# Applying the inverse softmax sum of grouped heads after the product with V, in place of before it

## Chip, cores and metric

One core of a Trainium2 chip runs the whole program. The metric is the device time of one execution in microseconds, the median of several runs. A profiled execution gives, beside its time, the start and duration of every instruction on the engines: TensorE (PE, and PEld for its weight loads), VectorE (DVE), ScalarE (ACT), GpSimd (POOL), and SyncE (SP), which issues most of the transfers.

## What is computed

Two layers of a block with four parallel head groups (pooling, grouped-query attention, a long convolution called hyena, latent attention), an output projection and a mixture of experts with 16 experts. There are 512 latent tokens and 256 context tokens. Latent queries read keys of both, 768 in all; context queries, in the first layer only, read the 256 of the context. The part that matters here is the attention:

```python
def attend(q, k, v, scale):
    s = jnp.einsum('bqhgd,bkhd->bhgqk', q, k).astype(jnp.float32) * scale
    p = jax.nn.softmax(s, axis=-1).astype(v.dtype)
    return jnp.einsum('bhgqk,bkhd->bqhgd', p, v)

# in reference(), for each layer: four query heads of 64 on two key/value heads
o_gqa = block_sweep_attention(gqa_q(p_q, gqa_qnorm_g[l], pos),
                              jnp.concatenate([kl, kc], axis=1), jnp.concatenate([vl, vc], axis=1), gqa_scale)
...
mixed = jnp.concatenate([o_pool, o_gqa, o_hy, o_mla], axis=-1) @ w_out[l]
```

## The kernel before

Everything is f32, and where a matmul is to be fast, an operand is split into a high and a low half in a faster type (`split`, L715 to L721: ACT copies the high half, L718, and DVE subtracts it from the source, L721).

**Attention.** `attention` runs the grouped heads (kind "g") first and the latent heads (kind "m") after them, in two pairs of heads each; for a pair it goes over blocks of 128 queries, six in layer 0 (four latent, two context) and four in layer 1. One block of one pair is the generator `attend`, in three steps, and `step` keeps three blocks in flight: a new block does its first step, the block before it the second, the one before that the third.

The first step, `probs`, runs for each of the two heads: the scores by matmul into PSUM (L1116, two tiles of 1024 columns shared with hyena), the negated row maximum on DVE (L1118), the exponential on ACT with the row sum as its second output (L1121), the reciprocal of the sum on DVE (L1122), and then the scaling of the whole tile of probabilities P, 128x768 for latent queries and 128x256 for context queries. `SCALE_BY` gives the engine of that scaling by the block's number and the head: for grouped heads "vvpppv", where v is DVE (L1127) and p is POOL (L1125). The second step, `probs_t`, transposes P in pieces of 128x128 on PE (L1139) and evacuates them by ACT (L1144) or DVE (L1142). The third, at the end of `attend`, multiplies with V (L1064): the two heads of a pair stand side by side in one PSUM tile `po`, at partitions 0 and 64, with twelve matmuls for a latent block and four for a context block. The result, 128 feature rows by 128 queries, is split straight from PSUM into the tiles `oT` (L718, L721), which the output projection reads much later.

**Beside it.** The hyena chains (`hyena_chain`) are advanced between the blocks of the grouped heads. Each goes through PE (L1195, L1218), ACT (L1198), DVE and POOL (products and sums L1200 to L1212, dealt out by `HYENA_BY`; L1203, L1205 and L1206 are on POOL, L1204, L1207 and L1208 on DVE) and back to PE, and the two chains alternate. The rest of the transposed operands (L1073) and, in layer 0, the modulation of the next layer (L367, L375) run between them as well.

**Order.** The order in the code is not the order on the engines: the tile framework's planner places the instructions of each engine by a simulated timeline, except where `in_order` ties PE's. Every engine then runs its own queue in order.

**What the change touches.** `SCALE_BY`, the end of `probs` (L1120 to L1130), and `attend`. The buffers: P has four, the sums `sm` six, the small PSUM tiles (`ps1`: transposes, `po`, hyena) four.

Of the kernel before, what the change touches and what calls it, by code (L numbers as in the profile page):

```python
# [10 lines left out]
F32 = mybir.dt.float32  # L11
F32R = mybir.dt.float32r
U32 = mybir.dt.uint32
AF = mybir.ActivationFunctionType
OP = mybir.AluOpType
# [162 lines left out]
EARLY = 3, 9  # L178
LATE_STEPS = ((1, 0), (1, 2), (2, 0), (2, 2))

SCALE_BY = dict(g="vvpppv", m="vvpvpp")
EVACUATE_BY = dict(g="avaa", m="aaaa")
HYENA_BY = "pvppvvvppp"

# [21 lines left out]
class Block:  # L206
# [844 lines left out]
    def attend(self, p, kind, pair, i, ks, qs):  # L1051
        nc = self.nc
        kb = range(6) if i < 4 else range(4, 6)
        heads = (2 * pair, 2 * pair + 1)
        P = {h: self.probs(p, kind, qs[h], ks[h], i, h % 2, kb)
             for h in heads}
        yield
        pts = {h: self.probs_t(p, P[h], len(kb), kind, h % 2) for h in heads}
        yield
        po = self.ps1()  # L1060
        for j, b in enumerate(kb):
            for x, h in enumerate(heads):
                v = self.G[:, b, 64 * pair:64 * pair + 64] if kind == "g" else self.MV[:, b, 64 * h:64 * h + 64]
                nc.tensor.matmul(po[64 * x:64 * x + 64, :128], v, pts[h][:, j, :], start=j == 0, stop=j == len(kb) - 1,  # L1064
                                 tile_position=(0, 64 * x))
        c = slice(128 * i, 128 * i + 128)
        ob = (2 if kind == "g" else 6) + pair
        self.split(self.oT[0][ob][:, c], self.oT[1][ob][:, c], po[:, :128])

    def t_raw(self, srcs, w):  # L1070
        pt = self.ps1()
# [34 lines left out]
    def probs(self, p, kind, q, k, i, x, kb):  # L1106
        nc = self.nc
        k0, n = 128 * kb[0], 128 * len(kb)
        S = self.ps2()
        c = slice(128 * i, 128 * i + 128)  # L1110
        K = 128 if kind == "g" else 96
        terms = ((0, 0), (0, 1)) if kind == "g" else ((0, 0), (0, 1), (1, 0))
        for y, (a, b) in enumerate(terms):
            for s in range(0, n, 512):
                e = min(s + 512, n)
                nc.tensor.matmul(S[:, s:e], q[a][:K, c], k[b][:K, k0 + s:k0 + e], start=y == 0, stop=y == len(terms) - 1)  # L1116
        nm = self.work.tile([128, 1], F32, name="nm", tag="nm", bufs=6)
        nc.vector.tensor_reduce(nm, S[:, :n], axis=AX.X, op=OP.max, negate=True)  # L1118
        P = p.tile([128, NT], F32, name="P", tag="P", bufs=4)
        sm = self.work.tile([128, 1], F32, name="sm", tag="sm", bufs=6)  # L1120
        nc.scalar.activation(P[:, :n], S[:, :n], AF.Exp, bias=nm, accum_out=sm)  # L1121
        nc.vector.reciprocal(sm, sm)  # L1122
        e = SCALE_BY[kind][(2 * i + x) % 6]
        if e == "p":
            nc.gpsimd.tensor_scalar(P[:, :n], P[:, :n], sm, 1.0, op0=OP.mult, op1=OP.mult)  # L1125
        elif e == "v":
            nc.vector.tensor_scalar(P[:, :n], P[:, :n], sm, None, op0=OP.mult)  # L1127
        else:
            nc.scalar.activation(P[:, :n], P[:, :n], AF.Copy, scale=sm)
        return P  # L1130

    def probs_t(self, p, P, nk, kind, h):
        nc = self.nc
# [571 lines left out]
```

## Time and profile before

| | us |
|---|---|
| median of three runs | 1486.69 |
| lowest and highest | 1483.56, 1487.9 |
| profiled execution, its time | 1484.3 |
| its span, first to last instruction | 1482.4 |
| mean granted TensorE clock | 0.952 |

The page gives busy time and shares by engine; the queries of the trace give them by stretch, by line and along the chain that ended last. In the chain each piece is the work, or the time of the engine's queue ("issue"), that released what came after it. A line number is that of the kernel printed above.

### The profile page before, as it was taken

To read this page: it belongs to the slowest core of one execution; us is meant where nothing else is said; L and a number is where in the kernel's file an instruction comes from. 1 tells how busy PE (TensorE), PEld (TensorE's weight loads), DVE (VectorE), ACT (ScalarE), POOL (GpSimd) and SP (SyncE) were. 2 spreads that over 40 slices of the span, in tenths; PEclk is the share of its full clock that TensorE was granted. 3 is DMA by queue.
4 is the path that set the end of the run, shared out by engine and by line. 5 is a ranking of instruction groups with operands and counts; after the bars stand their busy time and mean duration, and the time that the engine had idled before them with its cause. 6 is when DMAs were issued, how large, how long until landed. Compare 5 with 4: busy or idle time off the path is not lost.

```text
span 1482.4 us, 23909 instructions
## 1 busy us (share of the span) xinstructions
PE 1345.9 (91%) x9457; PEld 888.8 (60%) x9457; DVE 684.3 (46%) x1831; ACT 507.1 (34%) x1238; POOL 341.9 (23%) x360
## 2 busy tenths in 40 slices
PE   6999999888899998999999968988899974998896
PEld 2577787777678895444444437977778961332221
DVE  4656364687663547122222227585787452221111
ACT  4545333435564433111111136544357430111000
POOL 1510141254210115121222132042521011111101
PEclk9989999999899998999999989999999986999998
DMA  9546746011265139899999980123100858999996
GB/s 386 220 159 243 278 156 245 31 58 43 79 264 170 58 128 350 341 395 392 396 392 398 386 283 5 61 83 139 57 30 3 350 203 326 406 393 409 405 402 215
DMA packets 72737, 345.96 MB, mean 233 GB/s; under 512 B 7105, under 2 KB 23105, under 8 KB 38322
## 3 DMA queue, kind: packets, MB, share of 16 engines
q1 hardware_dynamic: 57488, 305.24, 52.3%
q0 software_dynamic: 13104, 32.19, 8.0%
q10 hardware_dynamic: 2034, 7.00, 1.2%
q8 instruction: 75, 1.23, 0.3%
q14 instruction: 36, 0.29, 0.1%
HBM read 317.70 MB, written 26.71 MB: 232 GB/s over the span
## 4 chain that ended last, share of the span: by engine, by line
PE 74%; DVE 9%; DMA 9%; ACT 3%; issue 3%; POOL 1%; POOLq 0%; ACTq 0%; DVEq 0%; SPq 0%
PE b L1622 13%; PE b L808 7%; PE b L1655 6%; PE b L1633 4%; PE b L1116 3%; PE b L367 3%; PE b L797 3%; PE b L798 3%; PE b L799 3%; PE b L1064 3%; DMA ring<-wu 3%; PE b L1304 3%; PE b L1306 3%; PE b L1305 3%; PE b L1139 3%
## 5 line engine op out<-in xcount | busy, mean ns | idle before, releaser
L1622 PE MATMUL b<-ring,xg 128*64 128x512 f32 x824 | 222.4, 618 | 13.5 <-DMA ring<-wu 10.6
L1622 PEld LDWEIGHTS b<-ring,xg 128*64 128x64 f32 x824 | 66.9, 141 | 130.5 <-issue 103.1
L1608 ACT ACTIVATE sgl<-b 64x512 f32<-64x512 f32 x32 | 18.9, 591 | 345.9 <-PE b L1622 345.9
L1655 PE MATMUL b<-ring,hTm 128*64 128x512 f32 x464 | 110.9, 605 | 2.0 <-DVE hTm L1649 1.3
L797 PE MATMUL b<-whi,hT 128*128 128x256 f32 (+1 forms) x352 | 103.1, 294 | 0.3 <-DVE h L769 0.3
L798 PE MATMUL b<-wlo,hT 128*128 128x256 f32 (+1 forms) x352 | 100.3, 285 | 0.0
L799 PE MATMUL b<-whi,hT 128*128 128x256 f32 (+1 forms) x352 | 99.9, 284 | 0.0
L1116 PE MATMUL b<-kop,qop 96*128 96x512 f32 (+3 forms) x360 | 86.1, 370 | 13.5 <-ACT P L1121 10.8
L808 PE MATMUL b<-hT,whi 128*128 128x512 f32 (+1 forms) x384 | 96.3, 357 | 1.5 <-DVE cv L864 1.3
L721 DVE TENSOR_TENSOR wlo<-ringt,whi 128x256 fp32r<-128x256 f32 (+1 forms) x192 | 83.0, 474 | 30.1 <-ACT whi L718 29.7
L1649 DVE COPY hTm<-b 128x384 f32<-128x384 f32 (+1 forms) x32 | 15.7, 491 | 164.0 <-PE b L1646 98.3
L718 ACT ACTIVATE whi<-ringt 128x256 fp32r<-128x256 f32 (+1 forms) x192 | 67.5, 404 | 47.6 <-PE b L808 22.4
L1601 POOL DMA_INDIRECT xs<-y,sidx x32 | 50.2, 1568 | 135.0 <-DVE y L1599 131.5
L1121 ACT ACTIVATE P<-b,nm 128x768 f32<-128x768 f32 (+1 forms) x80 | 65.4, 818 | 38.9 <-DVE nm L1118 37.2
L1118 DVE TENSOR_REDUCE nm<-b 128x1 f32<-128x768 f32 (+1 forms) x80 | 67.1, 845 | 23.1 <-PE b L1116 22.4
L797 PEld LDWEIGHTS b<-whi,hT 128*128 128x128 f32 x352 | 68.4, 195 | 12.3 <-issue 3.7
L1116 PEld LDWEIGHTS b<-kop,qop 96*128 96x128 f32 (+1 forms) x360 | 58.5, 201 | 25.2 <-ACT P L1121 14.0
L808 PEld LDWEIGHTS b<-hT,whi 128*128 128x128 f32 x384 | 63.2, 188 | 15.3 <-ACT oT L1263 2.1
L1304 PE MATMUL b<-whi,oT 128*128 128x256 f32 x240 | 71.3, 299 | 0.0
L798 PEld LDWEIGHTS b<-wlo,hT 128*128 128x128 f32 x352 | 68.7, 195 | 3.2 <-issue 2.5
L1655 PEld LDWEIGHTS b<-ring,hTm 128*64 128x64 f32 x464 | 32.7, 138 | 60.9 <-issue 57.4
L1144 ACT ACTIVATE PT<-b 128x384 f32<-128x384 f32 (+1 forms) x140 | 57.3, 448 | 34.4 <-PE b L1139 33.5
(398 smaller groups left out, 2881.1 us busy)
## 6 DMA issues: line engine op xcount, KB each, us to landing
ring<-wd SPq DMA_DIRECT2D x58, 1024.0 KB
ring<-wu SPq DMA_DIRECT2D x53, 1024.0 KB
ring<-wg SPq DMA_DIRECT2D x50, 1024.0 KB
ringt<-wmod SPq DMA_DIRECT2D x46, 1024.0 KB
ringt<-win SPq DMA_DIRECT2D x14, 1024.0 KB
ringt<-wg SPq DMA_DIRECT2D x14, 1024.0 KB
ringt<-wu SPq DMA_DIRECT2D x11, 1024.0 KB
ringt<-wout SPq DMA_DIRECT2D x8, 1024.0 KB
```

The costliest lines, as they stand in the source:

```text
L718: nc.scalar.activation(hi, src, AF.Copy)
L721: nc.vector.tensor_tensor(lo, src, hi.bitcast(F32), op=OP.subtract)
L797: nc.tensor.matmul(pt[:, :n], hT[0][:, k, t], hi[k], start=k == 0, stop=False)
L798: nc.tensor.matmul(pt[:, :n], hT[0][:, k, t], lo[k], start=False, stop=False)
L799: nc.tensor.matmul(pt[:, :n], hT[1][:, k, t], hi[k], start=False, stop=k == 7)
L808: nc.tensor.matmul(pt[:, a:b], w[k][:, cs], hT[h][:, k, a:b], start=first and k == 0, stop=end and k == 7)
L1116: nc.tensor.matmul(S[:, s:e], q[a][:K, c], k[b][:K, k0 + s:k0 + e], start=y == 0, stop=y == len(terms) - 1)
L1118: nc.vector.tensor_reduce(nm, S[:, :n], axis=AX.X, op=OP.max, negate=True)
L1121: nc.scalar.activation(P[:, :n], S[:, :n], AF.Exp, bias=nm, accum_out=sm)
L1304: nc.tensor.matmul(pt[:, :256], oT[0][k][:, t], hi[k], start=k == 0, stop=False)
L1622: nc.tensor.matmul(pa[64 * j:64 * j + 64], X[:, k, o:o + 64], w[k // 4][:, c], start=k == 0, stop=k == 7, tile_position=(0, 64 * j))
L1655: nc.tensor.matmul(py[64 * j:64 * j + 64], hT[:, f], wd[f // 2][:, d:d + 512], start=f == 0, stop=f == 3, tile_position=(0, 64 * j))
```

## The change

For grouped heads the probabilities stay as the exponential leaves them. `probs` returns the reciprocal of the sum beside P. After the product with V, one matmul a head writes the reciprocals, spread over 64 rows, into columns 128 to 255 of the same PSUM tile: the stationary operand is the column of 128 reciprocals repeated 64 times, the moving one the identity, so that each output row holds the reciprocals of the 128 queries. ACT copies that spread tile into SBUF (`rsb`), DVE multiplies the product with V by it into SBUF (`on`), and the split reads `on` in place of PSUM. The latent heads keep their scaling; their line of `SCALE_BY` has only v and p, so that the branch for ACT goes.

```diff
-SCALE_BY = dict(g="vvpppv", m="vvpvpp")
+SCALE_BY = "vvpvpp"
...
-        P = {h: self.probs(p, kind, qs[h], ks[h], i, h % 2, kb)
-             for h in heads}
+        P, sums = {}, {}
+        for h in heads:
+            P[h], sums[h] = self.probs(p, kind, qs[h], ks[h], i, h % 2, kb)
...
-        self.split(self.oT[0][ob][:, c], self.oT[1][ob][:, c], po[:, :128])
+        o = po[:, :128]
+        if kind == "g":
+            for x, h in enumerate(heads):
+                nc.tensor.matmul(po[64 * x:64 * x + 64, 128:256], sums[h].to_broadcast([128, 64]), self.ident,
+                                 start=True, stop=True, tile_position=(0, 64 * x))
+            r = p.tile([128, 128], F32, name="rsb", tag="rsb", bufs=2)
+            nc.scalar.activation(r, po[:, 128:256], AF.Copy)
+            o = p.tile([128, 128], F32, name="on", tag="on", bufs=2)
+            nc.vector.tensor_tensor(o, po[:, :128], r, op=OP.mult)
+        self.split(self.oT[0][ob][:, c], self.oT[1][ob][:, c], o)
...
-        sm = self.work.tile([128, 1], F32, name="sm", tag="sm", bufs=6)
+        sm = self.work.tile([128, 1], F32, name="sm", tag="sm", bufs=8)
...
-        e = SCALE_BY[kind][(2 * i + x) % 6]
+        if kind == "g":
+            return P, sm
+        e = SCALE_BY[(2 * i + x) % 6]
...
-        else:
-            nc.scalar.activation(P[:, :n], P[:, :n], AF.Copy, scale=sm)
-        return P
+        return P, sm
```

## Rows read from the trace of the kernel before

**Rows 1.** The page, busy time, share of the span and instructions of each engine.

```profile
PE 1345.9 (91%) x9457; PEld 888.8 (60%) x9457; DVE 684.3 (46%) x1831; ACT 507.1 (34%) x1238; POOL 341.9 (23%) x360
```

**Rows 2.** Stretches: us, busy and count of PE, PEld, DVE, ACT, POOL; granted clock, DMA.

```profile
280.00:320.00 40.00, 34.88 (x244) 30.95 (x243) 32.98 (x61) 19.45 (x41) 20.92 (x18) 0.91 0.09 27
320.00:360.00 40.00, 31.93 (x224) 26.95 (x223) 34.09 (x71) 15.51 (x44) 21.31 (x26) 0.92 0.24 79
360.00:400.00 40.00, 33.48 (x265) 28.39 (x264) 27.45 (x68) 20.29 (x56) 11.63 (x18) 0.87 0.08 28
400.00:440.00 40.00, 39.64 (x357) 29.47 (x357) 23.93 (x60) 28.17 (x75) 5.06 (x7) 1.00 0.68 260
...
1080.00:1100.00 20.00, 18.61 (x131) 16.15 (x131) 15.77 (x31) 12.09 (x28) 6.67 (x7) 0.83 0.16 54
1100.00:1120.00 20.00, 19.84 (x191) 17.08 (x192) 15.30 (x34) 14.65 (x37) 1.51 (x2) 1.00 0.01 2
```

**Rows 3.** Stretches, DVE scaling L1127 alone: us, busy and count, clock, DMA.

```profile
285.00:394.00 109.00, 7.86 (x12) 0.89 0.15 49
1040.00:1105.00 65.00, 7.15 (x10) 0.90 0.12 43
```

**Rows 4.** The same for the POOL scaling L1125.

```profile
300.00:392.00 92.00, 8.65 (x12) 0.91 0.16 53
1050.00:1098.00 48.00, 5.84 (x6) 0.93 0.13 45
```

**Rows 5.** The chain that ended last: start us, us, what.

```profile
299.11 0.54 DVE P L1127
...
327.19 1.42 issue
...
336.97 1.45 PE b L1064 x22
...
347.32 0.53 DVE P L1127
...
1046.74 0.54 DVE P L1127
...
1076.35 1.43 issue
...
1103.77 0.53 DVE P L1127
...
1117.05 1.46 PE b L1064 x24
```

**Rows 6.** Timeline, DVE and POOL: start us, us, engine, line, operation, tiles.

```profile
300.62 0.67 DVE L1207 TENSOR_TENSOR layt<-layt 128x512 f32<-128x512 f32 x1
...
327.06 1.63 DVE L1127 TENSOR_SCALAR P<-P,sm 128x768 f32<-128x768 f32 x1
328.24 1.57 POOL L1206 TENSOR_TENSOR layt<-layt 128x512 f32<-128x512 f32 x1
328.81 1.55 DVE L1207 TENSOR_TENSOR layt<-layt 128x512 f32<-128x512 f32 x1
...
354.88 2.06 POOL L1125 TENSOR_SCALAR P<-P,sm 128x768 f32<-128x768 f32 x2
355.03 1.02 DVE L1208 TENSOR_TENSOR layt<-layt 128x256 f32<-128x256 f32 x1
355.98 1.11 DVE L1211 TENSOR_TENSOR hyscr<-hyscr 128x128 f32<-128x128 f32 x2
357.88 0.48 DVE L1211 TENSOR_TENSOR layt<-layt 128x128 f32<-128x128 f32 x2
```

**Rows 7.** Groups by line and form, 285 to 412 us: busy us, mean ns, idle before.

```profile
L1118 DVE TENSOR_REDUCE nm<-b 128x1 f32<-128x768 f32 x24 | 22.6, 950 | 3.8 <-PE b L1116 3.5
...
L721 DVE TENSOR_TENSOR oT<-b,oT 128x128 fp32r<-128x128 f32 x12 | 3.4, 282 | 2.9 <-ACT oT L718 2.9
L718 ACT ACTIVATE oT<-b 128x128 fp32r<-128x128 f32 x12 | 3.3, 278 | 10.0 <-PE b L1064 10.0
```

More of the change, by code (lines that the diff above doesn't have):

```diff
@@ L1119, in probs @@
         P = p.tile([128, NT], F32, name="P", tag="P", bufs=4)
-        sm = self.work.tile([128, 1], F32, name="sm", tag="sm", bufs=6)
+        sm = self.work.tile([128, 1], F32, name="sm", tag="sm", bufs=8)
         nc.scalar.activation(P[:, :n], S[:, :n], AF.Exp, bias=nm, accum_out=sm)
         nc.vector.reciprocal(sm, sm)
-        e = SCALE_BY[kind][(2 * i + x) % 6]
+        if kind == "g":
+            return P, sm
+        e = SCALE_BY[(2 * i + x) % 6]
         if e == "p":
             nc.gpsimd.tensor_scalar(P[:, :n], P[:, :n], sm, 1.0, op0=OP.mult, op1=OP.mult)
-        elif e == "v":
+        else:
             nc.vector.tensor_scalar(P[:, :n], P[:, :n], sm, None, op0=OP.mult)
-        else:
-            nc.scalar.activation(P[:, :n], P[:, :n], AF.Copy, scale=sm)
-        return P
+        return P, sm
     def probs_t(self, p, P, nk, kind, h):
```

## The prediction

> **What bounds the kernel now.** I read the busy shares first [rows 1]: PE 91%, DVE 46%, ACT 34%, POOL 23%. An average over stages, it says only that whatever is put on PE is paid somewhere. The change touches the grouped heads, which run at about 290 to 406 us in layer 0 and 1035 to 1119 us in layer 1, so the second view is busy time by stretch [rows 2]. From 280 to 360 us DVE is busy 33 and 34 of 40 us while PE has 5 and 8 us idle: there DVE and the hyena chain, which shares its queue, set the pace. From 360 to 400 us PE idles 6.5 us, and from 400 us on PE is full. Layer 1 repeats it: 15.8 of 20 us of DVE with PE at 18.6 from 1080 to 1100 us, PE full from 1100 us. POOL is half busy at most. So the same microsecond is worth something on DVE early in the grouped heads and on PE late in them. What it is worth is read from the third view, the chain that ended last: a piece of work that isn't on it gives nothing when it goes.
>
> The grouped heads take 20 blocks (two pairs of heads, six blocks of queries in layer 0 and four in layer 1), 40 scalings in all.
>
> **Removed: 22 scalings on DVE.** They take 7.86 us (12) and 7.15 us (10), 15.0 us [rows 3]. On the chain stand only 11 of them: five in layer 0, 2.57 us together, and six in layer 1, 2.89 us (the first and the last of each layer in [rows 5]). Term: -5.5 us. With the order of the work unchanged this is also the most that their own time can give.
>
> One of the 22, at 327 us, ran beside POOL's hyena products and took 1.63 us in place of about 0.6; its like in layer 1 did the same, and the chain carries 1.42 and 1.43 us there as "issue" [rows 5, 6]. That wait goes too, but what is late next stands close by: POOL's product L1206 ends at 329.8 us and DVE's L1208 needs it, while L1207, the last piece ahead of L1208, ends at 330.4 now [rows 6]. So I take 0.5 us at each place, -1.0 us; ends 0 and -2.85.
>
> **Removed: 18 scalings on POOL.** 8.65 us and 5.84 us [rows 4], none on the chain. Their worth is what they slow on DVE: two of them at 354.9 to 356.9 us stand beside L1208 (1.02 us) and the pair L1211 (1.11 us) [rows 6]. The pair took 0.48 us when the scalings were over, 0.63 less, and I give L1208 as much. Both are on the chain: -1.2 us; ends 0 and -1.3. The reciprocal stays, and all waits around it.
>
> **Added on PE: two matmuls a block.** The stationary operand is the column of inverse sums spread over 64 columns, the moving one the identity, 128 columns, f32: the shape of the product with V. There a block of 12 matmuls shows as 24 instructions and lasts 1.46 us [rows 5], 61 ns each, with the two heads side by side in the array. Two more are four instructions, 0.244 us a block, 4.9 us for 20. The product with V is on the chain in 12 of the 20 blocks (nine pieces in layer 0, four in layer 1; the first and the last in [rows 5]): +2.9 us; ends 0, if they run in PE's gaps, and +4.9. A zero-stride stationary operand I price as any other.
>
> **Added on DVE: one product a block.** 128x128, one source in PSUM, as the subtraction of the split now: 282 ns [rows 7], 5.6 us for 20. I give it the chain share of what it replaces in the same queue, 5.5 of 15.0 or 36%: +2.0 us; ends +0.6 (about a tenth, which is what the existing subtractions have on the chain) and +5.6. Net, DVE has 15.0 - 5.6 = 9.4 us less to do.
>
> **Moved: the subtraction of the split.** It read PSUM and one SBUF tile; now it reads two SBUF tiles. No 128x128 row of that kind stands in these stretches; the nearest is L1207, two SBUF sources of 128x512, which took 0.67 us at 300.6 us, where POOL stood idle, and 1.55 us beside POOL's L1206 [rows 6], 0.9 more. The subtractions that stand beside or just ahead of hyena products are four (about 321, 329, 1070 and 1078 us). Term: four times 0.9 by a chain share between a tenth and 36%, the larger: +1.3, cut to +1.0 because a scaling that took the same wait is gone from two of these places; ends 0 and 4 x 1.57 = +6.3, a whole POOL product each.
>
> The Trainium skill, SBUF — State Buffer, section Who interferes with whom, says that a DVE instruction with two SBUF inputs contends with a GpSimd instruction that reads SBUF, that one of them then blocks for the other's whole instruction, and that with at most one SBUF input it doesn't contend outside the two-port modes. By that the subtraction loses a freedom that it has now, and the sum would take the upper end in place of +1.0. The rows agree in kind (L1207), and not that every such place costs a whole POOL instruction: 0.9 us of 1.57 there.
>
> **Added on ACT: one copy a block**, PSUM to SBUF, 278 ns as the copy of the split [rows 7], 5.6 us in all. ACT is busy 20 us or less of 40 to 400 us and 15 of 20 in the last stretch of layer 1 [rows 2], so I take 0; ends 0 and, with the 12 blocks of the chain, +3.3. The copy that makes the high half changes its source to SBUF and keeps 278 ns.
>
> **Added waits.** Before: PE, ACT copy, DVE subtraction. After: PE, ACT copy, DVE product, ACT copy, DVE subtraction. DVE's product waits for ACT where the subtraction waited before, so that costs nothing new. New is that the second ACT copy waits for the DVE product, and behind it in ACT's queue stand the next exponentials (L1121) and the evacuations of the transposed probabilities (L1144), for which PE waits. No such wait is in this trace; from 0 to one row maximum, 0.95 us [rows 7], a block. I take 0, since the planner puts work between such a pair, and keep the other end for a rival. The output tiles themselves are read only by the output projection, long after. The sums live two steps longer; eight buffers for the six alive leave no wait. No DMA is added or moved, and SP's queue is passed by nothing.
>
> **Sum.** -5.5 - 1.0 - 1.2 + 2.9 + 2.0 + 1.0 = -1.8 us. After the grouped heads PE is full through the other heads and the projection, and the expert loads of layer 1 start when the last attention tiles are free, so a gain is carried to the end. Against the profiled execution, 1484.3 us with a span of 1482.4, that is 1482.5; that execution lies 2.4 us under the median of the runs, 1486.7. Against the median it gives **1484.9 us**. All gains at their ends and PE's and DVE's additions at the low ones: -5.5 - 2.85 - 1.3 + 0.6 = -9.1, 1477.6 us.
>
> **Rivals.** *Relief in full.* DVE is the pace until PE's last long stall is over, about 380 us and 1092 us, so PE's additions fall into idle time until there, and of the 12 chain blocks only the eight later than that pay: 8 x 0.244 = 2.0. With DVE's product at its low end and no contention: -5.5 - 2.0 - 1.2 + 2.0 + 0.6 = -6.1, about 1480.5 us. For it: DVE at 84% beside PE at 80 to 87% [rows 2]. Against it: the scalings have only a third of their time on the chain.
> *Held ACT queue.* The second copy waits behind whatever DVE does. With one row maximum ahead of the product, 0.95 us, in the 12 chain blocks, at DVE's 84% busy: 12 x 0.95 x 0.84 = +9.6, net +7.8, about 1494.5 us, slower. It decides from about 0.55 us of held ACT in each of the 12 blocks (6.3 us, which takes back the 1.8 and costs 4.5). For it: the strict order of ACT's queue and DVE at 84% early. Against it: ACT idles half of the early stretch, and late DVE is at 69 to 77% [rows 2].
> *Port wait in full.* The subtraction at its upper end: -1.8 - 1.0 + 6.3 = +3.5, about 1490.2 us. The skill's rule above is this mechanism. Against it: four places of 20, and the planner can put them elsewhere.
> That the change doesn't do what it says has no case: the scalings go by a plain return.
>
> **How the numbers follow.** What a measurement here can tell from no change is about 0.3%, 4.5 us: faster is below 1482.2, slower above 1491.2. Forecast 0.44, with a range of its own of 1481 to 1488.5, of it 0.05 below 1482.2; relief in full 0.28, faster; held ACT 0.20, slower; port wait 0.08, same. Faster 0.05 + 0.28 = 0.33, same 0.39 + 0.08 = 0.47, slower 0.20. The range of 1478 to 1494 takes in the low end of the sum nearly and about half of the held queue, and leaves out some 0.1 to 0.15.
>
> **What would show it.** Right: scalings of grouped heads gone from DVE and POOL, 80 new PE instructions at about 61 ns apart; DVE from 280 to 360 us down from 67 to about 63 of 80 us; PE's idle from 280 to 400 us 1 to 3 us smaller; the grouped heads' last product with V at most 3 us earlier per layer. Wrong: an ACT gap of over 0.5 us ahead of the second copy in most blocks (held queue); subtractions of over 1 us (port); or a different order of hyena and attention, which moves PE's long stalls and the stretches at a granted clock of 0.87 to 0.92 [rows 2]: the planner sees other work and may place all of it anew, and no row of before prices that.

## The result and the profile after

The changed kernel takes 1494.8 us (median of six runs, 1490.4 to 1499.1) against 1484.5 us for the kernel before: a ratio of 1.0064, 95% interval 1.0046 to 1.0082. It is slower by 0.64%, and 0.8 us above the upper end of the predicted range. The profiled execution ran 1494.4 us with a span of 1492.6, 10.2 us more than that of before.

The page of the changed kernel: busy time of each engine (answers to [rows 1]), and the engines' shares of the chain that ended last.

```profile
PE 1351.9 (91%) x9537; PEld 893.3 (60%) x9537; DVE 675.9 (45%) x1829; ACT 512.4 (34%) x1258; POOL 328.4 (22%) x342
...
PE 69%; DMA 12%; DVE 10%; ACT 4%; issue 3%; POOL 1%; POOLq 0%; SPq 0%; ACTq 0%; DVEq 0%
```

DVE and POOL do less (8.4 and 13.5 us), PE has the 80 new instructions, ACT 20 copies more. The change does what it says. The stretches of [rows 2] in the changed kernel, with the columns given there:

```profile
280.00:320.00 40.00, 34.25 (x241) 30.49 (x240) 31.93 (x59) 19.99 (x42) 16.04 (x14) 0.91 0.09 27
320.00:360.00 40.00, 31.42 (x235) 26.41 (x234) 31.44 (x67) 16.69 (x47) 19.59 (x21) 0.91 0.23 79
360.00:400.00 40.00, 33.38 (x254) 28.84 (x253) 24.69 (x65) 19.00 (x54) 9.92 (x14) 0.83 0.08 27
```

From 280 to 360 us DVE fell from 67.1 to 63.4 of 80 us, as promised. But PE did not close up behind it: its idle time from 280 to 400 us is 20.95 us, and was 19.7.

To see where the 10 us came in, I measured four lengths in each trace: **A0** and **A1**, from the first score matmul to the first projection matmul of layers 0 and 1 (the attention stages, with the hyena chains); **T0**, from the last projection matmul of layer 0 to the first matmul of its experts (the routing, its last loads, the late filter); and **S**, from the first score matmul of layer 0 to the end. Single executions of one kernel spread by over 10 us (the kernel before ran between 1477.5 and 1492.6 us in one set of rounds), much of it ahead of the first score matmul and in the expert stages. Between the two traces that the kernels before and after each have, A0 and T0 differ by at most 0.3 us, A1 by at most 1.1. So the steps below are read from these lengths, and the ratio stands beside them. All kernels of the study, lengths in us from one trace each, ratio to the kernel before from 6 to 12 runs:

| kernel | A0 | T0 | A1 | S | ratio (95%) |
|---|---|---|---|---|---|
| before, two traces | 177.7, 177.4 | 37.5, 37.5 | 123.5, 122.4 | 1195.2, 1194.4 | 1.0014 (1.0000 to 1.0028) |
| after, two traces | 182.4, 182.3 | 42.9, 42.9 | 123.6, 123.6 | 1205.4, 1202.2 | 1.0064 and 1.0058 (1.0035 to 1.0081) |
| after_order_of_before | 178.7 | 41.4 | 123.0 | 1197.0 | 1.0023 (1.0000 to 1.0047) |
| before_order_of_after | 183.1 | 40.2 | 126.7 | 1208.5 | 1.0086 (1.0056 to 1.0116) |
| relief_in_order | 173.7 | 37.5 | 119.7 | 1183.7 | 0.9946 (0.9928 to 0.9964) |
| add_in_order | 180.0 | 39.4 | 125.5 | 1197.7 | 1.0021 (1.0004 to 1.0039) |
| psum_in_after_order | 183.7 | 45.2 | 124.6 | 1204.9 | 1.0071 (1.0042 to 1.0099) |
| psum_in_order | 179.0 | 37.9 | 122.3 | 1193.5 | 1.0015 (0.9997 to 1.0034) |
| after_tail_of_before | 182.0 | 41.9 | 123.5 | 1200.2 | 1.0036 (1.0016 to 1.0055) |
| before_tail_of_after | 177.4 | 40.5 | 122.3 | 1193.5 | 0.9992 (0.9973 to 1.0012) |
| after_pe_order | 179.7 | 39.5 | 122.6 | 1201.6 | 1.0060 (1.0040 to 1.0079) |
| after_dve_order | 179.1 | 40.5 | 126.4 | 1198.1 | 1.0059 (1.0032 to 1.0085) |
| after_hyena_order | 182.5 | 41.4 | 123.5 | 1203.9 | 1.0083 (1.0052 to 1.0113) |
| before_other_split | 177.9 | 39.8 | 124.6 | 1198.0 | 1.0025 (1.0009 to 1.0041) |
| rec_in_order | 184.2 | 37.4 | 125.2 | 1204.1 | 1.0041 (1.0018 to 1.0063) |
| rec_free | 181.4 | 40.3 | 124.9 | 1202.5 | 1.0077 (1.0048 to 1.0106) |
| early_in_order | 187.3 | 40.2 | 127.3 | 1209.1 | 1.0088 (1.0064 to 1.0112) |

The kernel before against itself came out at 1.0014 (up to 1.0028), so a ratio of that size tells nothing. The second line is the loss: A0 +4.8, T0 +5.4, A1 +0.7 against the means of before, and 0.8 us given back in the experts of layer 0 (from their first matmul to the last of the main down projection 274.3 us, against 274.8 and 275.3). Half of it lies in T0, where not one instruction was edited. But the lengths don't all arrive at the end: before_tail_of_after has 3.0 us more in T0 than before and the time of before (0.9992, S 1193.5), and after_pe_order has 2.7 and 3.4 us less in A0 and T0 than the changed kernel and its ratio (1.0060).

### The profile page after: what moved, and what is told of

It is laid out like the page before. It is cut to its first block, busy times and chain, and to the rows that moved or that the text cites. A ratio compares the mean times of both kernels' runs of the same rounds, so it can differ in the third digit from the quotient of the medians.

```text
span 1492.6 us, 24054 instructions
## 1 busy us (share of the span) xinstructions
PE 1351.9 (91%) x9537; PEld 893.3 (60%) x9537; DVE 675.9 (45%) x1829; ACT 512.4 (34%) x1258; POOL 328.4 (22%) x342
## 4 chain that ended last, share of the span: by engine, by line
PE 69%; DMA 12%; DVE 10%; ACT 4%; issue 3%; POOL 1%; POOLq 0%; SPq 0%; ACTq 0%; DVEq 0%
PE b L1632 10%; PE b L808 7%; PE b L1665 5%; DMA ring<-wg 4%; PE b L1643 4%; DMA ring<-wu 4%; PE b L1126 3%; PE b L367 3%; PE b L1065 3%; PE b L797 3%; PE b L798 3%; PE b L799 3%; PE b L1149 3%; PE b L1314 2%; PE b L1315 2%
## 5 line engine op out<-in xcount | busy, mean ns | idle before, releaser
L1632 PE MATMUL b<-ring,xg 128*64 128x512 f32 x824 | 217.5, 605 | 16.4 <-DMA ring<-wu 12.5
L1126 PE MATMUL b<-kop,qop 96*128 96x512 f32 (+3 forms) x360 | 84.1, 366 | 13.2 <-ACT P L1131 11.1
L797 PEld LDWEIGHTS b<-whi,hT 128*128 128x128 f32 x352 | 68.5, 195 | 12.4 <-issue 3.7
L1128 DVE TENSOR_REDUCE nm<-b 128x1 f32<-128x768 f32 (+1 forms) x80 | 66.8, 844 | 19.6 <-PE b L1126 18.8
L1126 PEld LDWEIGHTS b<-kop,qop 96*128 96x128 f32 (+1 forms) x360 | 57.9, 199 | 24.2 <-ACT P L1131 13.6
L799 PEld LDWEIGHTS b<-whi,hT 128*128 128x128 f32 x352 | 68.6, 195 | 0.8 <-issue 0.8
```

What stands on the lines that cost most here:

```text
L797: nc.tensor.matmul(pt[:, :n], hT[0][:, k, t], hi[k], start=k == 0, stop=False)
L799: nc.tensor.matmul(pt[:, :n], hT[1][:, k, t], hi[k], start=False, stop=k == 7)
L1632: nc.tensor.matmul(pa[64 * j:64 * j + 64], X[:, k, o:o + 64], w[k // 4][:, c], start=k == 0, stop=k == 7, tile_position=(0, 64 * j))
```

## The experiments

Three theories stand against each other. **Theory 1**: the planner, seeing other work, places untouched instructions anew, and that order costs the time. **Theory 2**: the subtraction of the split, now with two SBUF operands, waits beside POOL. **Theory 3**: the second ACT copy, waiting for DVE's product, holds ACT's queue.

**Order apart from work.** Both kernels share all instructions but the 40 scalings and the new ones, and write them down in the same sequence before the planner sorts them. So the order that it gave to one kernel can be held in the other, by order-only dependencies along each engine's list; the instructions that only one kernel has are left to the planner.

```diff
+                end = self.replay(f"A{l}")
                 self.attention(l, pp, ag, hy, hyena_done, mla_out, last, side)
                 side.drain()
+                end()
...
+            for e, runs in REPLAY.get(key, {}).items():
+                order = [own[e][a + j] for a, k in runs for j in range(k)]
+                for prev, i in zip(order, order[1:]):
+                    self.tc.add_manual_dep(i, prev.name, mybir.DependencyInfo(
+                        mybir.DependencyClass.NoSync, mybir.DependencyReason.DATA), reason="in order")
```

REPLAY holds the lists as runs (first place in the written sequence, count), for the attention stages of both layers (A0, A1) and for the stretch from the projection of layer 0 to its experts (P0).

> The changed kernel with the instructions that both kernels have held in the order of the kernel before on PE, DVE, ACT and POOL, in the attention stages of both layers and in the stretch between projection and experts of layer 0; only the new instructions (spread, copy, product) are placed by the planner. What is left is the price of the change's own instructions and waits. Theory 1 (order is most of the loss): close to my sum, 1483 to 1487, ratio 0.999 to 1.0015. Theory 2 (the subtraction with two SBUF sources waits beside POOL, 2.3 us in layer 0, and PE's own additions of 0.24 us per block for about ten blocks where PE is full): 1487 to 1490, ratio 1.0015 to 1.0035. Theory 3 (the second ACT copy holds ACT's queue, in 20 blocks): the whole loss of the grouped-head stages stays whatever the order, and the time is that of the run with the tail's order alone, 1489 to 1492, ratio 1.003 to 1.005.

> The kernel before, with its own scalings of the probabilities and none of the new instructions, but with all other instructions of the attention stages and of the stretch behind the projection of layer 0 in the order of the changed kernel on PE, DVE, ACT and POOL. Theory 1: it is as slow as the changed kernel or nearly so, 1490 to 1495, ratio 1.0037 to 1.007. Theories 2 and 3, by which the new instructions themselves cost the time: 1484 to 1486 if only the tail is neutral too, and at most 1490 with the tail's 5.3 us.

The first came out at 1.0023, the second at 1.0086. The attention stage of layer 0 in both kernels (columns as in [rows 2]), the changed kernel in the order of before first:

```profile
288.40:467.00 178.60, 157.24 (x1314) 128.97 (x1313) 120.00 (x280) 97.31 (x268) 52.74 (x64) 0.94 0.33 116
```

```profile
283.70:466.80 183.10, 158.44 (x1267) 129.73 (x1265) 124.41 (x282) 95.12 (x257) 62.44 (x76) 0.92 0.32 114
```

The second kernel has the work of before, to the instruction (PE x1267, POOL x76), and is 5.6 us longer in A0 than the kernel before, by order alone; the first has the work of the changed kernel (x1314) and is 1.1 us longer than before. Theory 1 stands for A0: of its 4.8 us, 3.7 are order. In layer 1 the order of after costs 3.7 us with the work of before, and 0.6 us with the work of the changed kernel. No run holds a kernel in its own order without another edit, so what the holding costs by itself isn't measured; the nearest is psum_in_after_order below, with A0 1.3 us longer than in the changed kernel.

How the order costs can be read from A0 of the changed kernel and of the kernel before (second trace):

```profile
287.20:469.70 182.50, 160.88 (x1316) 132.36 (x1314) 120.81 (x280) 98.20 (x267) 53.94 (x64) 0.92 0.32 114
282.60:460.00 177.40, 156.99 (x1267) 128.53 (x1265) 123.16 (x280) 94.78 (x255) 62.21 (x76) 0.93 0.33 117
```

In the changed kernel PE is busy for 160.9 us in its own order and for 157.2 in the order of before, with the same matmuls, while its idle time is the same within 0.3 us. What differs is the granted clock: 27.4 us of A0 lie at 0.50 (1.2 GHz, the lower of its two levels) in the one, 21.1 in the other. So the 3.7 us are not longer waits but slower work; 6.3 us more at half speed are worth about 3.2 us of work, an estimate from these rows. In us, two traces averaged where there are two:

| kernel | A0 | PE busy | PE idle | of A0 at 0.50 |
|---|---|---|---|---|
| before | 177.5 | 157.1 | 20.4 | 23.9 |
| after | 182.4 | 160.7 | 21.7 | 27.4 |
| after_order_of_before | 178.7 | 157.3 | 21.4 | 21.1 |
| before_order_of_after | 183.1 | 158.5 | 24.7 | 28.5 |
| relief_in_order | 173.7 | 154.4 | 19.2 | 20.5 |
| add_in_order | 180.0 | 157.4 | 22.6 | 18.8 |

With the work of before, the other order costs mostly idle time (4.3 of 5.6 us). That the clock is the way in which the order costs is read from traces; no run changed the clock alone.

**The two halves of the change, in the order of before.**

```diff
-        if kind == "g":
-            with self.added():
-                for x, h in enumerate(heads):
...
-                nc.vector.tensor_tensor(o, po[:, :128], r, op=OP.mult)
```

> The changed kernel without spread, copy and product, so that the grouped heads stay unnormalised; all other instructions held in the order of the kernel before in the attention stages of both layers and behind the projection of layer 0. It measures the removed scalings by themselves. My sum has 7.7 us for them (5.5 on the chain, 1.0 beside POOL, 1.2 of slowed hyena steps). If they were on the path: ratio 0.994 to 0.997, and the two grouped-head stretches together 6 to 8 us shorter than 177.7 + 123.5 us. If the hyena chain or the fixed order of PE ends each step anyway: ratio 0.9985 to 1.001, and the stretches at most 2 us shorter.

```diff
-        if kind == "g":
-            return P, sm
-        e = SCALE_BY[(2 * i + x) % 6]
+        e = SCALE_BY[kind][(2 * i + x) % 6]
+        with self.added() if kind == "g" else ExitStack():
```

> The changed kernel with the old scalings kept as well, so that the grouped heads are normalised twice; all instructions of the kernel before held in its order. It measures spread, copy, product and the split from two SBUF sources by themselves. My sum: +5.9 us (2.9 PE, 2.0 DVE, 1.0 subtraction), ratio 1.003 to 1.005, upper end with the port wait in full +11, ratio 1.0075. If an instruction placed in a fixed order mostly falls into idle time: +1 to +3 us, ratio 1.0005 to 1.002. If the held ACT queue matters (the second copy of ACT behind DVE's product, 20 blocks): idle time of ACT before that copy of over 0.5 us a block and a ratio of 1.005 or more.

The two stages of the first (removal alone), then of the second (additions alone):

```profile
283.10:456.80 173.70, 154.46 (x1268) 126.60 (x1266) 115.51 (x268) 94.98 (x255) 53.37 (x64) 0.94 0.34 120
1023.20:1143.00 119.80, 109.66 (x936) 95.06 (x934) 85.33 (x166) 71.51 (x172) 34.84 (x32) 0.96 0.15 51
```

```profile
287.40:467.40 180.00, 157.43 (x1315) 128.79 (x1313) 125.72 (x292) 97.97 (x269) 61.48 (x76) 0.95 0.33 116
1034.70:1160.20 125.50, 113.55 (x967) 97.97 (x966) 93.98 (x184) 73.93 (x179) 40.38 (x38) 0.95 0.18 62
```

The removal gives 3.9 + 3.2 = 7.1 us, the additions cost 2.5 + 2.6 = 5.1 us. That is my sum, nearly: 7.7 and 5.9. Added up they make -2.0 us, but both together, in the same order, came to +1.1 in A0 and +0.1 in A1. So 3.2 us don't add, 2.5 of them in A0. The table above shows where: PE's idle time does add (-1.2 and +2.2 make +1.0, and +1.0 was measured); its busy time doesn't (-2.7 and +0.3 against +0.2), since removal and additions, each alone, also shortened the time at the lower clock level, by 3.4 and 5.1 us, and both together by only 2.8. So in this place most of what the removal alone, and the additions alone, seem to be worth is the clock that they met.

**The port wait.** In the changed kernel DVE's product and subtraction in layer 0 stand as follows (count, then least, median and most ns):

```profile
L1077 DVE TENSOR_TENSOR on<-b,rsb x12: 276/282/292, 319.3 to 412.7; 128x128 f32<-128x128 f32 x12
L721 DVE TENSOR_TENSOR oT<-on,oT x12: 277/282/1374, 321.0 to 414.4; 128x128 fp32r<-128x128 f32 x12
```

Two subtractions took 1.37 and 1.34 us beside POOL's hyena products; in the kernel before they took 0.28 [rows 7]. With the product in PSUM one of its operands leaves SBUF:

```diff
-                o = p.tile([128, 128], F32, name="on", tag="on", bufs=2)
+                o = po[:, 256:384]
```

> The changed kernel in its own order (held on PE, DVE, ACT and POOL in the attention stages and behind the projection of layer 0), with one edit: DVE writes its product into PSUM, so that the subtraction of the split reads one operand from SBUF and not two. In the traces of the changed kernel that subtraction took 1.37 and 1.34 us in place of 0.28, twice in layer 0, while POOL worked on the hyena tables. Theory 2 (the port wait costs up to 2.3 us of the 4.8 that the grouped-head stage of layer 0 grew by): the two long subtractions fall to about 0.28 us and the stage from 182.4 to 180 to 180.5 us. If the wait lies beside other work, and order is the cause: the long subtractions go, the stage stays at 181.7 to 182.6 us, ratio 1.004 to 1.007.

> The changed kernel with the product in PSUM as in the run beside it, and the shared instructions held in the order of the kernel before, as in the run with the order of before (178.7 us in the stage of layer 0, 123.0 in that of layer 1, 41.4 behind the projection; 177.7, 123.5 and 37.5 in the kernel before). There the subtraction was lengthened three times, to 0.7 us. Theory 2: 0.5 to 1.5 us less over both stages. If it is beside other work: the same within 0.3 us. Ratio 0.999 to 1.002, and the stretch behind the projection anywhere from 37.5 to 42 us, since it goes by where a DVE operation meets one of POOL there.

The same line in the changed kernel's own order, with the product in PSUM:

```profile
L772 DVE TENSOR_TENSOR oT<-b,oT x12: 276/281/292, 323.0 to 417.8; 128x128 fp32r<-128x128 f32 x12
```

The long subtractions are gone, all 12 under 0.3 us, and A0 is 183.7 us, not shorter than 182.4. In the order of before the same edit changes A0 by +0.3 and A1 by -0.7. Theory 2 falls. Yet both waits stand on the changed kernel's chain that ended last:

```profile
321.08 1.30 DVE oT L721
...
330.28 1.27 DVE oT L721
```

With the product in PSUM the next hyena step on DVE comes no sooner, since it waits for POOL's product, or is slowed beside POOL itself:

```profile
324.31 0.69 DVE L1270 TENSOR_TENSOR hyscr<-hyscr 128x512 f32<-128x512 f32 x1 [0.98 <-POOL hyscr L1268]
...
333.47 1.74 DVE L1270 TENSOR_TENSOR layt<-layt 128x512 f32<-128x512 f32 x1 [0.31 <-POOL layt L1268]
```

The first of these steps starts 35.0 us behind the first score matmul, and 35.1 in the changed kernel; the second takes 1.74 us in place of 0.68. The wait for POOL is there either way, on one instruction or on the next: standing on the chain is not yet a price.

**The held ACT queue** needs no run of its own. ACT's waits for DVE's product in A0 (us in total, times, longest), in the changed kernel:

```profile
ACT oT L718 <- DVE on L1077: 4.8, 5, 1.8
```

and in the changed kernel in the order of before:

```profile
ACT oT L769 <- DVE on L1129: 10.8, 12, 2.5
```

The kernel with more than twice the wait, 0.9 us in each of 12 blocks, has the shorter stage, by 3.7 us. So Theory 3 falls as the cause of the loss. What these waits are worth beside the 1.1 us that are left in the order of before, no run took apart.

**Which place of the order.** Three kernels hold part of it: PE alone; DVE, ACT and POOL alone; and 74 PE instructions around the second round of the hyena chains.

```diff
+REPLAY = {"A0": {"PE": [(99, 3), (114, 4), (75, 1), (102, 4), (76, 6), (142, 16), (106, 4), (118, 12), (158, 9), (130, 12), (167, 3)]}}
```

(the last of the three is shown, the others hold the whole lists of their engines in A0 and A1)

> The changed kernel with PE alone held in the order of the kernel before, in the attention stages of both layers; DVE, ACT and POOL are placed by the planner. It tells which engine's order cost the stage of layer 0 its 3.7 us (182.4 us in the planner's order, 178.7 in the order of before on all engines). If PE's order does (scores and transposes of heads put ahead of hyena's transforms, or behind them): 178.5 to 179.5 us. If the order of DVE, ACT and POOL does: 181.5 to 183 us. Between the two if both take part.

> The changed kernel with DVE, ACT and POOL held in the order of the kernel before, in the attention stages of both layers; PE is placed by the planner. If the order of these three engines cost the 3.7 us: 178.5 to 179.5 us in the stage of layer 0. If PE's order did: 181.5 to 183 us.

> The changed kernel with 74 PE instructions of layer 0 held in the order of the kernel before, and nothing else: those around the second round of the hyena chains. In the traces the changed kernel has the hyena product that opens this round ready 1.6 us earlier than the kernel before, and its transform on PE then starts 2.0 us later, since the planner put scores, transposes and AV matmuls of the attention ahead of it. If this place is where the order costs the stage of layer 0 its 3.7 us: 178.7 to 180 us (182.4 in the changed kernel, 178.7 with the whole order of before, 179.7 with PE's whole order). If the loss is spread over the later re-placements: 181.5 to 182.5 us.

The place looked plain in the traces. PE in the changed kernel, from the product that closes the first hyena round (start us, us, line, operation, tiles; L1195 transposes the chain's input, L1205 is its transform, L1126 scores, L1149 transposes of the probabilities):

```profile
304.39 3.66 PE L1228 MATMUL b<-ringt,layt 128*128 128x256 f32 x14 [0.49 <-DVE layt L1221]
307.70 1.05 PE L1126 MATMUL b<-kop,qop 128*128 128x512 f32 x4
308.59 0.49 PE L1149 MATMUL b<-cst,P 128*128 128x128 f32 x3
308.91 0.64 PE L1195 MATMUL b<-cst,cv 128*128 128x128 f32 x4
310.30 2.27 PE L1205 MATMUL b<-hyscr,ringt 128*128 128x128 f32 x18 [0.75 <-ACT hyscr L1196]
312.42 0.63 PE L1195 MATMUL b<-cst,cv 128*128 128x128 f32 x4
312.89 1.15 PE L1149 MATMUL b<-cst,P 128*128 128x128 f32 x9
313.87 1.73 PE L1205 MATMUL b<-hyscr,ringt 128*128 128x128 f32 x14
```

The changed kernel in the order of before (here L1247, L1257, L1178 and L1201; its first score matmul is 1.1 us later):

```profile
306.48 0.59 PE L1280 MATMUL b<-ringt,layt 128*128 128x256 f32 x2
306.91 0.63 PE L1247 MATMUL b<-cst,cv 128*128 128x128 f32 x4
307.38 2.76 PE L1280 MATMUL b<-ringt,layt 128*128 128x256 f32 x12
309.97 3.73 PE L1257 MATMUL b<-hyscr,ringt 128*128 128x128 f32 x32
```

The transform of the second round ends at 315.60 us in the one, 313.70 in the other: counted from the first score matmul 28.4 and 25.3 us. In the one, four scores and three transposes of the attention stand ahead of the round and nine transposes inside it; in the other it runs through. Yet holding this place alone brought nothing (A0 182.5), since DVE and POOL stood in the new order and the later rounds lost as much. Holding PE's whole order brought 2.7 us of 3.7, holding that of the other three 3.3. The loss isn't one misplaced group; either engine's order, held, pulls most of the rest along. Neither made the program faster than the changed kernel (1.0060 and 1.0059); the order of all engines, in all three stretches, did (1.0023). After_dve_order is 2.8 us longer in A1 than the changed kernel.

**The stretch behind the projection.** Two kernels run once more with no edit, and two exchange their order in this stretch alone:

```diff
+REPLAY = {
+    "P0": {
...
+        "Pool": [(0, 1), (2, 1), (1, 1), (3, 12), (17, 3), (22, 5), (15, 1), (27, 1), (16, 1), (28, 3), (20, 2)],
```

> The kernel before once more, with no edit, for a second trace. In its first trace the stretch from the last projection matmul of layer 0 to the first matmul of the experts took 37.5 us; in five other kernels of this study it took 40.2 to 42.9, in whatever order it stood. Theory A, 37.5 is this kernel's own length and the change adds 3 to 5 us there by something that is not the order: 37 to 38.5 us again. Theory B, the length of this stretch differs from one execution to the next and the first trace was a short one: 39 to 42 us, and the median of the timed runs as for the kernel before, ratio 0.998 to 1.002.

> The changed kernel once more, with no edit, on the chip and in the rounds of the others, so that all ratios stand against the same runs. Expected of both theories: ratio 1.005 to 1.008; in the trace the stretch from the first score matmul to the first projection matmul of layer 0 takes 182 to 183 us again (177.7 in the kernel before). By theory B on the stretch behind the projection, its 42.9 us may come out anywhere from 39 to 43.

> The changed kernel, with one thing fixed: between the output projection and the experts of layer 0 each engine's instructions stand in the order that the planner gave them in the kernel before (they are the same instructions in both kernels; in the changed kernel the planner pulled one POOL scaling of xh ahead of three sums of the late filter, and two PE transposes ahead of eight matmuls of it). In the traces this stretch is 5.3 us longer after the change, although nothing in it is edited. Theory 1, the re-placed order of untouched work costs these 5.3 us: the time comes down from 1494.8 to 1489.5 (1488.5 to 1490.5), a ratio of about 1.0034 to the kernel before. Rival, the stretch is longer because it starts later and meets other transfers or another clock, whatever its order: 1494 to 1496, ratio 1.0064 to 1.0075.

> The kernel before, unchanged, except that the stretch between projection and experts of layer 0 is held in the order that the planner gave it in the changed kernel. Theory 1: that order alone costs 5.3 us, 1484.5 + 5.3 = 1489.8 (1488.5 to 1491), ratio about 1.0036. Rival (the length of the stretch comes from its start, transfers or clock): 1484 to 1485.5, ratio 0.9995 to 1.0007.

Theory A holds: 37.5 us is the kernel's own length, 42.9 the changed kernel's. But order explains only part: after's order costs the kernel before 3.0 us, and before's order gives the changed kernel 1.0 back, and in the table T0 is anything from 37.4 to 45.2. And for the whole program the first came out near its rival (0.9995 to 1.0007), at 0.9992, where the order theory had 1.0036.

A wait stands at the start of it. In the kernel before, second trace, DVE, then PE (L1470 to L1473 prepare two small tiles, L1477 and L1478 transpose them):

```profile
573.63 1.14 DVE L1470 COPY vals<-vals 32x64 f32<-32x64 f32 x1
574.70 1.32 DVE L1472 CAST idf<-idx 32x128 f32<-32x128 uint32 x1
576.06 1.04 DVE L1473 TENSOR_SCALAR idf<-idf,cst 32x128 f32<-32x128 f32 x1
```

```profile
575.82 1.48 PE L543 MATMUL b<-ones,ring 128*128 128x1 f32 x12
577.23 0.24 PE L1477 MATMUL b<-cst,vals 32*128 32x32 f32 x1
...
578.40 1.09 PE L1590 MATMUL b<-cst,graw 128*128 128x128 f32 x8
```

And in the changed kernel, POOL, DVE, PE:

```profile
585.39 1.28 POOL L534 TENSOR_TENSOR ring<-ring 128x512 f32<-128x512 f32 x1
586.62 1.27 POOL L536 TENSOR_TENSOR ring<-ring 128x512 f32<-128x512 f32 x1
```

```profile
584.84 3.13 DVE L1483 TENSOR_SCALAR idf<-idf,cst 32x128 f32<-32x128 f32 x1
```

```profile
588.03 0.24 PE L1488 MATMUL b<-cst,idf 32*128 32x32 f32 x1 [1.10 <-DVE idf L1483]
588.21 2.81 PE L543 MATMUL b<-ones,ring 128*128 128x1 f32 x16
...
591.90 1.97 PE L1600 MATMUL b<-cst,graw 128*128 128x128 f32 x8
```

In before_tail_of_after the same instruction is short, and the copy ahead of it has the wait:

```profile
575.65 2.82 DVE L1508 COPY vals<-vals 32x64 f32<-32x64 f32 x1
...
578.64 0.30 DVE L1511 TENSOR_SCALAR idf<-idf,cst 32x128 f32<-32x128 f32 x1
```

What takes 0.30 us there takes 3.13 in the changed kernel, and ends 0.08 us after the second of POOL's two. PE, whose next instruction needs it, stands for 1.10 us, and all 16 matmuls of L543 come after it in place of ahead of it. The Trainium skill, SBUF — State Buffer, section Who interferes with whom, names copy, cast and tensor_scalar as DVE operations that can take the ports which it shares with GpSimd, and says that whichever comes second then blocks for the whole of the other's instruction. The 3.13 us agree in kind, and go past two of POOL's instructions.

The wait is not what makes T0 long. Granted clock soon after this place (the clock is the number ahead of the DMA share) in the changed kernel, in the changed kernel in the order of before, and in the kernel before, second trace:

```profile
590.00:598.00 8.00, 7.50 (x33) 6.92 (x34) 3.75 (x15) 2.03 (x5) 4.51 (x5) 0.50 0.93 328
```

```profile
586.00:596.00 10.00, 9.50 (x43) 8.94 (x43) 4.16 (x16) 3.22 (x6) 4.36 (x5) 0.50 0.99 377
```

```profile
580.00:584.00 4.00, 3.20 (x15) 3.13 (x15) 2.82 (x8) 1.83 (x4) 3.68 (x4) 0.57 0.91 314
```

From 590 to 598 us PE is at 0.50 of full speed, its lower level of 1.2 GHz, and its eight matmuls of L1600 take 1.97 us in place of 1.09. In the order of before it is there as long, some 10 us, though there the three DVE instructions took 0.16, 0.22 and 0.38 us and PE waited for 0.32 us at most ahead of the fall; in the kernel before it is there for some 3 us. In all 19 traces T0 goes by the length of this last fall: some 3 us with a T0 of 37.4 to 37.9, some 7 with 39.4 to 41.9, some 10 with 41.4 to 42.9, and some 14 with 45.2. What sets it, order, the phase between DVE and POOL, or something else, no run took apart.

**A work-neutral edit.** If the planner's order is worth microseconds by itself, an edit that exchanges equal scalings between DVE and POOL should move the time as well.

```diff
-SCALE_BY = dict(g="vvpppv", m="vvpvpp")
+SCALE_BY = dict(g="vvvppp", m="vvpvpp")
```

> The kernel before with DVE and POOL changing places on one third of the scalings of the grouped heads (three of six stay on each), the rest placed by the planner. The work is the same in sum. Theory 1 (what an edit does to the planner's order is worth several us by itself): the stages move by 1 to 5 us in either direction, and the stretch behind the projection lies anywhere from 37.5 to 45 us. If the placement of untouched work were robust: within 1 us of 177.5, 37.5 and 123 us, ratio 0.999 to 1.001.

A0 moved by +0.3, T0 by +2.3 and A1 by +1.7 us against the means of before. Only T0 is well beyond what two traces of one kernel differ by, and the ratio, 1.0025 (1.0009 to 1.0041), can't be told from the 1.0014 (1.0000 to 1.0028) of the kernel before run once more. So this run doesn't show that a work-neutral edit costs time.

**Cheaper forms of the change.** Since the removal alone is worth 7.1 us, I tried two ways to pay less for what is put in its place: inverting the spread tile on DVE, and spreading ahead of the AV matmuls.

```diff
-        nc.vector.reciprocal(sm, sm)
         if kind == "g":
             return P, sm
+        nc.vector.reciprocal(sm, sm)
...
-                nc.scalar.activation(r, po[:, 128:256], AF.Copy)
-                o = p.tile([128, 128], F32, name="on", tag="on", bufs=2)
+                nc.vector.reciprocal(r, po[:, 128:256])
+                o = po[:, 256:384]
```

> An attempt at a cheaper form of the change, in the order of the kernel before: the sums are spread as they are, DVE inverts the spread tile out of PSUM (in place of two small inversions in front of it and of ACT's copy), and writes its product into PSUM. DVE does about as much as before (0.28 us for two times 0.15), ACT 20 copies of 0.28 us less, and the spread no longer waits for an inversion. With the product in PSUM alone the stages took 179.0 and 122.3 us. If the hop over ACT is on the path: 177 to 178.5 and 121 to 122, ratio 0.998 to 1.000. If PE's four instructions per block are what costs: as with the product in PSUM, within 0.5 us, ratio 1.000 to 1.003.

> The same cheaper form with every instruction placed by the planner. By theory 1 its order and with it its time is a draw: the stage of layer 0 anywhere from 177 to 184 us, the stretch behind the projection from 37 to 45, ratio 0.997 to 1.007. If its own work decided, it would lie within 1 us of the run in the order of before.

```diff
+        if kind == "g":
+            with self.added():
+                for x, h in enumerate(heads):
...
+                nc.scalar.activation(r, po[:, 128:256], AF.Copy)
         for j, b in enumerate(kb):
             for x, h in enumerate(heads):
...
                 o = po[:, 256:384]
                 nc.vector.tensor_tensor(o, po[:, :128], r, op=OP.mult)
```

> The changed kernel in the order of the kernel before, with the product in PSUM and with the spread and its ACT copy issued ahead of the attention's AV matmuls instead of behind them, so that the product can follow the last AV matmul at once. The removed scalings gave 7.0 us over the two stages when they were taken away alone; the additions took back 4.9 to 8. If the hop over ACT behind the AV matmuls is what costs beside PE's own 0.24 us a block: 177 to 178 us in layer 0 (179.0 with the product in PSUM alone) and 121 to 122 in layer 1, ratio 0.998 to 1.0005. If only PE's instructions cost: 178.5 to 179.5 and 122 to 123, ratio 1.000 to 1.003.

All three came out above the kernel before, and rec_in_order (1.0041) least clearly. Inversion of the tile, count and ns:

```profile
L1127 DVE RECIPROCAL rsb<-b x20: 939/957/959, 316.5 to 1127.4; 128x128 f32<-128x128 f32 x20
```

It takes 0.96 us, over three times a product of that size (0.29), in the middle of DVE's busiest stretch. And in early_in_order the AV matmuls wait for the ACT copy, with which they share a PSUM tile and no data; a run with two tiles was not made (load and matmul, us, times, longest):

```profile
PEld b L1123 <- ACT rsb L1119: 13.8, 12, 2.2
...
PE b L1123 <- ACT rsb L1119: 10.9, 12, 1.9
```

About 1 us of PE in each of 12 blocks: A0 187.3. Neither beats the kernel before; the nearest, the product in PSUM with the order of before held, is no faster than it (1.0015, 0.9997 to 1.0034).

## Why the prediction was wrong, by its own steps

- **The step that failed** is the sum's tacit condition, "with the order of the work unchanged", and the way the range was made from it. The last sentence of the prediction names the case ("the planner sees other work and may place all of it anew, and no row of before prices that"), and the stretches at a lower clock with it, and gives it neither a time, nor a chance, nor a share of the range. In A0 it was worth 3.7 of 4.8 us, and the traces show these as 6.3 us more at the lower clock level, for which the sum has no term either. With the order of before held on all engines the ratio fell from 1.0064 to 1.0023. T0, which the prediction doesn't look at, grew by 5.4; how much of that the order does, and how much of it arrives at the end, is open. That the range missed by only 0.8 us says little: some 5 us either way, the size of the order's effect in A0, would have held the result.
- **Removed scalings:** forecast -7.7 (5.5 + 1.0 + 1.2), measured alone -7.1. The size is right in a fixed order, the way is not that of the terms: in A0 2.7 of the 3.9 us are PE's busy time, with 3.4 us less of the stage at the lower clock level, and only 1.2 its waits.
- **Added work:** forecast +5.9, measured alone +5.1. The size was near. The zero-stride spread is no dearer than a plain matmul (start us, us, line; the changed kernel, then the kernel before):

```profile
410.62 0.66 PE L1065 MATMUL b<-PT,rowsG 128*64 128x128 f32 x8
411.11 0.39 PE L1072 MATMUL b<-cst,sm 128*64 128x128 f32 x4
411.42 0.66 PE L375 MATMUL b<-cst,part 128*128 128x128 f32 x4
```

```profile
405.96 0.66 PE L1064 MATMUL b<-PT,rowsG 128*64 128x128 f32 x8
406.55 0.66 PE L375 MATMUL b<-cst,part 128*128 128x128 f32 x4
```

From the first AV matmul to L375 it is 0.80 us with the spread and 0.59 without, 0.21 us a block or 4.2 us for 20, at the full clock, where I priced 4.9. DVE's product (282 ns) and ACT's copy (278 ns) came as priced.
- **The sum:** -1.8 forecast; +1.2 measured with the order held (A0 +1.1, A1 +0.1), though the two halves by themselves make -2.0. That terms add was the second assumption, off by 3.2 us; in A0 it failed in PE's busy time, with the clock.
- **Port wait:** its size was right for the upper end's kind (1.37 and 1.34 us in place of 0.28, where I had 1.57 for a whole POOL instruction), at two places and not four; its price was not: 0, by the runs that take it away, since the next step meets POOL in its place. The prediction also says that no 128x128 row with two SBUF sources stands in these stretches; L1211 in [rows 6] is one, and its pair took 1.11 us beside POOL and 0.48 without.
- **Held ACT queue:** its time, 1494.5, is almost the one measured, and it is not the cause. By my own condition it decides from 0.55 us in each of 12 blocks; with 0.9 us in each of 12 the stage is 3.7 us shorter than with 4.8 us in five blocks. That its time comes so near is chance.
- **Signs:** DVE from 280 to 360 us went to 63.4, as promised. PE's idle time rose by 1.2 us in place of falling by 1 to 3, and the last AV matmuls of the grouped heads in layer 0 came 4.7 us later in place of up to 3 earlier (410.62 us, in the rows above, against 405.96 in the trace of before). These two signs told of a different order, the sign that the prediction lists last.
- **What stays open:** why the new order leaves PE longer at the lower clock level, in A0 and in T0, and how much of T0's 5.4 us is order. Orders exchanged gave +3.0 and -1.0, which don't agree.

## What to carry to other kernels

Where a planner places the instructions, the price of an edit has two parts, its own work and the re-placement of everything near it; in the edited stage the second was 3.7 us here, against 1.1 us for the first, so give it a term of the range of its own. To learn what an edit is worth, hold the shared instructions in the old order and measure it there, halves apart, and look at the granted clock before the halves are added up: here PE's idle times added and its busy times didn't. A wait that stands on the chain has a price only if what comes next is free to start: taking DVE's wait beside POOL away brought nothing, since the next step waited for POOL too. And compare the time at the lower clock level behind the edited stage: T0 grew with it by up to 8 us, with no instruction of it edited.

## What the hardware showed that I had not expected

- DVE's RECIPROCAL of a 128x128 tile out of PSUM took 957 ns, where a product of that size took 291.
- A TENSOR_SCALAR of 32x128 with one tile in SBUF took 0.30 us in one kernel and 3.13 in another, where it stood beside two POOL products and ended 0.08 us after the second.
- The same matmuls of A0 took 3.5 us more of PE's busy time in one order than in another, with 27.4 and 21.1 us of the stage at the lower clock level. Eight matmuls at that level took 1.97 us in place of 1.09.
- Four matmul instructions with a zero-stride stationary operand of 64 columns lengthened a group of plain ones by 0.21 us, 53 ns each.
